# Two hybrid mixer layers on one core: the later modulations computed on VectorE, the neighbourhood projection computed transposed, and buffers redistributed

## The chip, the cores and the metric

One Trainium2 chip; the program runs on one of its cores. The time is device microseconds of one execution, and 2924.19 us is the median of three executions of the kernel before (2923.29 to 2927.37). The engines are named as in the profile: PE is TensorE (matmuls; PEld is its weight load), DVE is VectorE, ACT is ScalarE, POOL is GpSimd, SP is SyncE, which here only issues DMAs. Each engine runs its own instruction list strictly in the order in which it was written.

## The reference, cut to what matters

Two layers over 1024 latent tokens and 256 context tokens, width 1024, all in float32. In each layer:

```python
shift, scale, gate = split(silu(c) @ w_mod + b_mod, 3)      # once for c, once for c_ctx
p = (layer_norm(x) * (1 + scale) + shift) @ w_in            # latent and context tokens
ya = neighbourhood_attention(q_a, k_a, v_a, ...)            # q_a, k_a, v_a are columns of p
yb = latent_attention(...); yc = two_way_linear_scan(...); yd = grouped_query_attention(...)
acc = sum(sigmoid(m[i]) * ((y[i] * silu(z[i])) @ w_branch[i]) for i in range(4))
x = layer_norm(alpha * x + gate * (acc @ w_out)) * ln_g + ln_b
```

The modulation is a product of two vectors (c and c_ctx) with a 1024 x 3072 matrix per layer. Context rows are carried through the first layer only, and the last output is the latent stream.

## The kernel before, in words

Every large matmul is done three times on numbers split into a high and a low part (`whi`/`wlo` for weights, `xh`/`xl` for tokens; `mm_a` keeps the tokens stationary, lines 299 to 301, `mm_b` the weights, lines 307 to 309). `xh` and `xl` hold the normalized, modulated tokens transposed, 8 chunks of 128 channels by 1280 tokens, throughout a layer. `groups` are the token columns 0:256 (context), 256:768 and 768:1280; `qgroups` leaves the context out in layer 1.

A layer has these stages, which give the prefixes of the names in the profile: `g_proj`, `m_proj`, `a_proj` (projections for the three attentions, parts written to DRAM), `lru` (woven into `m_proj` and `a_proj`), `g_att`, `m_att`, `a_att` (attention, with half of the merge gates computed in between and kept in DRAM, name `gates`), `merge`, `outp`. In the trace, layer 0 has `a_proj` from about 255 to 380 us, attention from 410 to 1080, `merge` from 1080 to 1470 and `outp` to 1620; layer 1 has them from 1845 to 1957, 1957 to 2540, 2540 to 2815 and to the end.

Of the modulations, one half of layer 0 is computed at the start, and three pieces are computed beside the merge of layer 0 (prefix `mod`; `later_mods`, line 1165): the gate of layer 0 (1024 columns), shift and scale of layer 1 (2048) and its gate (1024). `modulation` loads `w_mod` in 64 tiles of 128 x 512 (`wm`, tag `q`, three buffers, line 185) and multiplies each on PE in plain float32 with the two conditioning vectors `sc` as a stationary operand of two columns (line 188), gathers over the 8 chunks in PSUM, copies the rows out and transposes them (line 197). `weave` interleaves these steps with those of `merge` in the program's text by shares (line 1011).

`a_steps` (line 801) makes q and k of the neighbourhood attention token tile by token tile, ten tiles of 128 tokens by 512 columns; ACT copies the product out of PSUM into `tmp` (lines 808, 809, q scaled by 0.125), and `put_t` (line 343) transposes four blocks of it on PE (line 348), splits them (`hi_lo`, lines 312 and 313) and writes them to DRAM.

In attention, `values` (line 574) transposes blocks of the probabilities on PE (line 584, PSUM tile `t`), splits them into `ph` (ACT, line 312) and `pl` (DVE, line 313), and multiplies both with the values (lines 591 and 592), two blocks behind (`AHEAD`). Tag `ph` has three buffers, tag `pl` two. `put_u` (line 438) spreads the reciprocal row sums with POOL into `rb` (line 448, one buffer), transposes that on PE (line 464) and multiplies it in. `tmp` is a tag of three buffers that nearly every stage uses. `spare` (line 128) takes buffers of `tmp`, `ph` and `pl` in turn for the residual rows in `outp`.

A scheduling layer below the kernel decides the order in which each engine's instructions finally stand; the order of the text and the buffers are its input.

Of the kernel before, what the change touches and what calls it, by code (L numbers as in the profile page):

```python
# [8 lines left out]
F32 = mybir.dt.float32  # L9
F32R = mybir.dt.float32r  # L10
# [7 lines left out]
KC = D // 128  # L18
# [15 lines left out]
G_LAG = 1  # L34
X_ACT = (0, 2)
M_ORDER = (2, 3, 1, 0)
W_A = 30
W_B = 48
Z_0, GATE_0 = 2, 10
UNITS = [(2, 3), (5, 3), (8, 2)]  # L40
# [7 lines left out]
def hybrid_kernel(ctx: ExitStack, tc, a):  # L48
# [79 lines left out]
    def spare():  # L128

        turns[0] += 1  # L130
        tag = ("tmp", "ph", "tmp", "pl", "tmp", "ph", "pl")[turns[0] % 7]
        return tp.tile([128, 512], F32, tag=tag, name=nm("spare"), bufs=2 if tag == "pl" else 3)

    def bank():
        turns[0] += 1
# [37 lines left out]
    def modulation(l, base, ncols, out, stage, sw):  # L173

        acc = ps_v.tile([128, 512], F32, tag="pv", name=nm("pm"))
        g = 4
        w_ = ncols // g
        n = ncols // 128
        bm = lc.tile([128, 16], F32, tag="bm", name=nm("bm"))
        sp.dma_start(bm[:, :n], a["b_mod"][l, :, base // 128:base // 128 + n])  # L180
        for k in range(KC):
            for h in range(ncols // sw):
                w = stage()
                c0 = base + h * sw
                sp.dma_start(w, a["w_mod"][l, k * 128:(k + 1) * 128, c0:c0 + sw])
                for j in range(sw // w_):
                    q = 32 * (h * sw // w_ + j)
                    pe.matmul(acc[q:q + 2, :w_], sc[:, k, :], w[:, j * w_:(j + 1) * w_],
                              start=k == 0, stop=k == KC - 1)
                yield  # L190
        tps = tbank()
        for j in range(g):
            row = tmp()
            act.copy(row[0:2, :w_], acc[32 * j:32 * j + 2, :w_])
            for i in range(w_ // 128):
                c = j * (w_ // 128) + i
                pe.transpose(tps[:, 2 * c:2 * c + 2], row[0:2, i * 128:(i + 1) * 128], ident[0:2, 0:2])
        mc = lc.tile([128, 2, 16], F32, tag="modc", name=nm("modc"), bufs=4)
        dve.tensor_tensor(mc[:, :, :n].rearrange("p s n -> p n s"),
                          tps[:, :2 * n].rearrange("p (n s) -> p n s", s=2),  # L200
                          bm[:, :n, None].to_broadcast([128, n, 2]), ALU.add)
        if n == 16:
            dve.tensor_scalar(mc[:, :, 8:16], mc[:, :, 8:16], 1.0, None, ALU.add)
        out["m"] = mc
        yield
# [109 lines left out]
    def layer(l, xh, xl, need_ctx, gate, finish, side, ahead=None):  # L315
# [27 lines left out]
        def put_t(dst, t, first, src):  # L343
# [6 lines left out]
            lo = tp.tile([128, 4, 128], F32R, tag="pl", name=nm("tl"), bufs=2)  # L350
# [87 lines left out]
        def put_u(i, c, y, rcp=None):  # L438
# [4 lines left out]
            for g in qgroups:  # L443
                gs = slice(g[0], g[0] + g[1])
                if rcp is not None:
                    r = tp.tile([128, 512], F32, tag="rb", name=nm("rb"), bufs=1)
                    t0, n = g[0] // 128, g[1] // 128
                    pool.tensor_copy(r[:, :g[1]].rearrange("p (t h e) -> p t h e", t=n, h=2),
                                     rcp[:, :, t0:t0 + n].rearrange("p h t -> p t h")[:, :, :, None]
                                     .to_broadcast([128, n, 2, 64]))  # L450
# [123 lines left out]
        def values(o, y, qts, blocks, pts, vt):  # L574
# [5 lines left out]
            def turn(vb, q0, cols):  # L580
# [2 lines left out]
                for i, col in enumerate(cols):  # L583
                    pe.transpose(tb[:, i * 128:(i + 1) * 128], pts[q0 + i][:, col:col + 128], ident)  # L584
                ph = tp.tile([128, 512], F32R, tag="ph", name=nm("ph"), bufs=3)
                pl = tp.tile([128, 512], F32R, tag="pl", name=nm("pl"), bufs=2)
                hi_lo(ph[:, :w], pl[:, :w], tb[:, :w])
                return vb, slice(128 * q0, 128 * q0 + w), ph[:, :w], pl[:, :w]

# [121 lines left out]
        def m_steps():  # L711
# [25 lines left out]
            def second(t, has_q, y, kr):  # L737
# [5 lines left out]
                cl = tp.tile([128, 512], F32R, tag="pl", name=nm("cl"), bufs=2)  # L743
# [56 lines left out]

        def a_steps():
            wa = load_rows(w_in, C_A, 512)
            prev = None
            for t, ps in project(wa, lambda t: 0 if t >= q0t else 256, 512):
                c0 = 0 if t >= q0t else 256
                y = tmp()
                if c0 == 0:
                    act.activation(y[:, :256], ps[:, :256], AF.Copy, scale=0.125)
                act.copy(y[:, 256:], ps[:, 256:])
                if prev:  # L810
                    put_t(*prev)
                prev = qk_a, t, c0 // 128, [y[:, c:c + 128] for c in range(c0, 512, 128)]
                yield
            put_t(*prev)
# [193 lines left out]

        for _ in fill["gen"]:
            pass  # L1010
        weave((f"merge{l}", merge(), 4 * KC * len(qgroups)), (f"mod{l}", side, 68))


        phase[0] = f"last{l}"
# [144 lines left out]
    ctx.push(pools)  # L1159
    x1 = dr.tile([SEQ, D], F32, name="x1", bufs=1)  # L1160

    def raw_w():
        return tp.tile([128, 512], F32, tag="q", name=nm("wm"), bufs=3)
# [107 lines left out]
```

## Time and profile before

| What | Value |
|---|---|
| median of three executions | 2924.19 us |
| the profiled execution | 2926.0 us, span 2924.2 us |
| mean granted TensorE clock | 0.979 of 2.4 GHz |
| PE busy | 2782.2 us, 95% of the span |
| DVE busy | 1503.1 us, 51% |
| ACT busy | 1219.3 us, 42% |
| POOL busy | 420.1 us, 14% |
| HBM traffic | 102 GB/s over the span |

A PE matmul is pipelined: its recorded duration (0.40 us for 512 columns) is longer than the distance to the next start (0.23 us), so costs on PE are read from starts. An idle time is what an engine stood still just before an instruction, with the instruction that released it. PEld waits are those of weight loads, which run ahead of the matmuls and may be hidden.

### The profile page before, as it was taken

The page shows a single profiled execution, that of the slowest core. Times are in us where ns is not written, and L with a number is a line of the kernel's source. Part 1 is how long each engine was busy: PE and PEld are TensorE (multiplying, and loading weights), DVE is VectorE, ACT ScalarE, POOL GpSimd, SP SyncE. Part 2 cuts the span into 40 slices and gives each one's busy share as a digit, 9 for nine tenths or more (in the row PEclk, how much of TensorE's full clock was granted, in tenths as well). Part 3 has the DMA queues.
Part 4 walks back from the last instruction along what each step waited for, and adds up shares of the span by engine and source line. Part 5 has one row for each costly group of instructions (what it writes and reads, how often), then busy time and mean ns, then how long its engine had stood idle before and what let it go on. Part 6 is the DMA issues. An engine that isn't in the chain of part 4 may idle for free. (4 is left out here: it accounts for less than half of the span.)

```text
span 2924.2 us, 40179 instructions
## 1 busy us (share of the span) xinstructions
PE 2782.2 (95%) x14458; PEld 2248.4 (77%) x14458; DVE 1503.1 (51%) x3085; ACT 1219.3 (42%) x2617; POOL 420.1 (14%) x507
## 2 busy tenths in 40 slices
PE   7978999999999999999999797999999999999998
PEld 4766788888888887777767586788888888777776
DVE  5645435555455652233358655445555556533357
ACT  4353535445455552222224435535545455522230
POOL 1211011110111100111222121011111111001131
PEclk9988999999999999999999898999999999999999
DMA  7424232222223324333332333342222333222232
GB/s 249 119 66 146 79 103 84 85 85 85 92 86 124 103 94 128 100 121 120 122 89 87 99 102 102 105 122 87 85 88 78 113 115 110 93 87 88 89 113 88
DMA packets 240424, 301.83 MB, mean 103 GB/s; under 512 B 27488, under 2 KB 160096, under 8 KB 240224
## 3 DMA queue, kind: packets, MB, share of 16 engines
q1 hardware_dynamic: 134368, 225.58, 24.5%
q10 hardware_dynamic: 105856, 73.68, 8.1%
q8 instruction: 114, 1.87, 0.3%
q14 instruction: 86, 0.70, 0.1%
HBM read 217.11 MB, written 82.07 MB: 102 GB/s over the span
## 5 line engine op out<-in xcount | busy, mean ns | idle before, releaser
L307 PE MATMUL merge__mm<-xh,merge__whi 128*128 128x512 f32 (+1 forms) x640 | 242.2, 378 | 0.9 <-ACT a_att__tmp L934 0.9
L308 PE MATMUL merge__mm<-xl,merge__whi 128*128 128x512 f32 (+1 forms) x640 | 238.6, 373 | 0.0
L309 PE MATMUL merge__mm<-xh,merge__wlo 128*128 128x512 f32 (+1 forms) x640 | 238.5, 373 | 0.0
L313 DVE TENSOR_TENSOR m_att__pl<-m_att__t,m_att__ph 128x384 fp32r<-128x384 f32 (+1 forms) x248 | 122.0, 508 | 117.5 <-ACT m_att__ph L312 78.8
L1005 DVE TENSOR_TENSOR merge__tmp<-wide,merge__tmp 128x512 f32<-128x512 f32 (+1 forms) x120 | 76.5, 637 | 194.8 <-PE wide L309 173.7
L263 ACT CAST merge__whi<-merge__wraw 128x256 fp32r<-128x256 f32 (+1 forms) x128 | 65.8, 514 | 249.3 <-PE merge__mm L308 172.9
L1006 POOL TENSOR_TENSOR merge__acc<-merge__acc,merge__tmp 128x512 f32<-128x512 f32 (+1 forms) x60 | 79.0, 1317 | 574.8 <-DVE merge__tmp L1005 574.7
L313 DVE TENSOR_TENSOR g_att__pl<-g_att__t,g_att__ph 128x384 fp32r<-128x384 f32 (+1 forms) x228 | 112.8, 515 | 88.3 <-ACT g_att__ph L312 56.0
L312 ACT CAST m_att__ph<-m_att__t 128x384 fp32r<-128x384 f32 (+1 forms) x248 | 105.2, 440 | 115.0 <-PE m_att__t L584 105.3
L307 PEld LDWEIGHTS merge__mm<-xh,merge__whi 128*128 128x128 f32 x640 | 120.2, 188 | 42.8 <-issue 16.5
L264 DVE TENSOR_TENSOR merge__wlo<-merge__wraw,merge__whi 128x256 fp32r<-128x256 f32 (+1 forms) x128 | 72.0, 563 | 131.8 <-ACT merge__whi L263 124.8
L309 PEld LDWEIGHTS merge__mm<-xh,merge__wlo 128*128 128x128 f32 x640 | 120.3, 188 | 23.8 <-issue 0.4
L308 PEld LDWEIGHTS merge__mm<-xl,merge__whi 128*128 128x128 f32 x640 | 120.3, 188 | 22.4
L307 PE MATMUL wide<-merge__uh,merge__whi 128*128 128x256 f32 (+1 forms) x320 | 127.9, 400 | 9.3 <-DVE merge__tmp L1005 6.7
L312 ACT CAST g_att__ph<-g_att__t 128x384 fp32r<-128x384 f32 (+1 forms) x228 | 98.2, 446 | 83.3 <-PE g_att__t L584 78.7
L307 PE MATMUL a_att__mm<-xh,a_att__whi 128*128 128x512 f32 (+1 forms) x320 | 123.7, 387 | 0.0
L641 DVE TENSOR_SCALAR_CACHE_REDUCE g_att__p<-wide 128x1280 f32<-128x1280 f32 (+1 forms) x72 | 98.6, 1369 | 45.9 <-PE wide L639 35.7
L641 DVE TENSOR_SCALAR_CACHE_REDUCE m_att__p<-wide 128x1280 f32<-128x1280 f32 (+1 forms) x72 | 98.7, 1371 | 42.3 <-PE wide L639 41.8
L309 PE MATMUL a_att__mm<-xh,a_att__wlo 128*128 128x512 f32 (+1 forms) x320 | 120.0, 377 | 0.0
L308 PE MATMUL a_att__mm<-xl,a_att__whi 128*128 128x512 f32 (+1 forms) x320 | 120.0, 375 | 0.0
L308 PE MATMUL wide<-merge__ul,merge__whi 128*128 128x256 f32 (+1 forms) x320 | 119.7, 374 | 0.0
L299 PE MATMUL a_proj__mm<-a_proj__whi,xh 128*128 128x256 f32 (+1 forms) x320 | 110.3, 346 | 9.9 <-ACT a_proj__whi L263 9.8
(418 smaller groups left out, 7908.4 us busy)
## 6 DMA issues: line engine op xcount, KB each, us to landing
merge__wraw<-in_w_chunks_dram SPq DMA_DIRECT2D x64, 256.0 KB, 2.9
mod__wm<-in_w_mod_dram SPq DMA_DIRECT2D x64, 256.0 KB, 3.1
g_proj__wm<-in_w_mod_dram SPq DMA_DIRECT2D x16, 512.0 KB, 9.6
a_att__wraw<-in_w_chunks_dram SPq DMA_DIRECT2D x32, 256.0 KB, 2.8
merge__wraw<-in_w_branch_dram SPq DMA_DIRECT2D x64, 128.0 KB, 2.0
merge__tmp<-start__gates SPq DMA_DIRECT2D x32, 256.0 KB, 3.2
merge__tmp<-outp__gates SPq DMA_DIRECT2D x32, 256.0 KB, 3.4
g_att__wraw<-in_w_chunks_dram SPq DMA_DIRECT2D x28, 256.0 KB, 2.7
```

The lines of the kernel that those rows point to most:

```text
L263: act.copy(hi[:, :n], raw[:, :n])
L264: (pool if by_pool else dve).tensor_sub(lo[:, :n], raw[:, :n], hi[:, :n])
L299: pe.matmul(ps, xh, wh[:, n0:n1], start=first and k == 0, stop=False)
L307: pe.matmul(ps, wh, xh, start=first and k == 0, stop=False)
L308: pe.matmul(ps, wh, xl, start=False, stop=False)
L309: pe.matmul(ps, wl, xh, start=False, stop=last and k == nk - 1)
L312: act.copy(hi, src)
L313: dve.tensor_sub(lo, src, hi)
L641: dve.tensor_scalar(pt[:, :nk], wide[:, :nk], -scale, None, ALU.mult, ALU.min, accum_out=nb)
L1005: dve.tensor_mul(sgm[:, :g[1]], pb[:, :g[1]], sgm[:, :g[1]])
L1006: (pool if w is None else dve).tensor_add(acc[c][:, gs], acc[c][:, gs], sgm[:, :g[1]])
```

## The change

`modulation_apart` replaces `modulation` for the three pieces beside the merge of layer 0 (the piece at the start stays). Each tile of `w_mod` is multiplied on DVE by the two conditioning vectors, one number per partition each, and added into two 128 x 512 sums, which take buffers of tags `ph` and `pl`; after eight tiles, eight matmuls with a single moving column of constants (-0.5) add up the partitions. Sum and factor -2 put the result in the layout that was reached by transposes before. `a_steps` computes q and k transposed at once, weights stationary, for each block of 128 columns and each token group, and splits them directly out of PSUM. Tag `pl` gets a third buffer; `rb` becomes a buffer of `tmp`. The weaving shares change (`W_A`, 68 to 76).

```diff
-W_A = 30
+W_A = 32
-        return tp.tile([128, 512], F32, tag=tag, name=nm("spare"), bufs=2 if tag == "pl" else 3)
+        return tp.tile([128, 512], F32, tag=tag, name=nm("spare"), bufs=3)
+    def modulation_apart(l, base, ncols, out):
+        acc = ps_v.tile([128, 512], F32, tag="pv", name=nm("pm"))
+        n = ncols // 128
+        bm = lc.tile([128, 16], F32, tag="bm", name=nm("bm"))
+        sp.dma_start(bm[:, :n], a["b_mod"][l, :, base // 128:base // 128 + n])
+        for h in range(ncols // 512):
+            sums = [tp.tile([128, 512], F32, tag=tag, name=nm("ms"), bufs=b) for tag, b in (("ph", 3), ("pl", 3))]
+            for k in range(KC):
+                w = raw_w()
+                sp.dma_start(w, a["w_mod"][l, k * 128:(k + 1) * 128, base + h * 512:base + (h + 1) * 512])
+                for s in range(2):
+                    if k == 0:
+                        dve.tensor_scalar(sums[s], w, sc[:, k, s:s + 1], None, ALU.mult)
+                    else:
+                        dve.scalar_tensor_tensor(sums[s], w, sc[:, k, s:s + 1], sums[s], ALU.mult, ALU.add)
+                yield
+            for s in range(2):
+                for c in range(4):
+                    o = s * n + 4 * h + c
+                    pe.matmul(acc[:, o:o + 1], sums[s][:, c * 128:(c + 1) * 128], mhalf[:, 0:1], start=True, stop=True)
+            yield
...
-                pl = tp.tile([128, 512], F32R, tag="pl", name=nm("pl"), bufs=2)
+                pl = tp.tile([128, 512], F32R, tag="pl", name=nm("pl"), bufs=3)
-                    r = tp.tile([128, 512], F32, tag="rb", name=nm("rb"), bufs=1)
+                    r = tmp()
...
             wa = load_rows(w_in, C_A, 512)
-            prev = None
-            for t, ps in project(wa, lambda t: 0 if t >= q0t else 256, 512):
-                c0 = 0 if t >= q0t else 256
-                y = tmp()
-                if c0 == 0:
-                    act.activation(y[:, :256], ps[:, :256], AF.Copy, scale=0.125)
-                act.copy(y[:, 256:], ps[:, 256:])
-                if prev:
-                    put_t(*prev)
-                prev = qk_a, t, c0 // 128, [y[:, c:c + 128] for c in range(c0, 512, 128)]
+            items = [(c, g) for c in range(4) for g in (qgroups if c < 2 else groups)]
+            def part(c, g, ps, ks):
+                xs = xs_g(g)
+                ws = [(wh[:, c * 128:(c + 1) * 128], wl[:, c * 128:(c + 1) * 128]) for wh, wl in wa]
+                mm_b(ps[:, :g[1]], [ws[k] for k in ks], lambda j: xs(ks[j]), ks[0] == 0, ks[-1] == KC - 1)
+            def keep(c, g, ps):
+                n, scale = g[1], 0.125 if c < 2 else 1.0
+                hi = tp.tile([128, 512], F32R, tag="ph", name=nm("th"), bufs=3)
+                lo = tp.tile([128, 512], F32R, tag="pl", name=nm("tl"), bufs=3)
+                act.activation(hi[:, :n], ps[:, :n], AF.Copy, scale=scale)
+                dve.scalar_tensor_tensor(lo[:, :n], ps[:, :n], scale, hi[:, :n], ALU.mult, ALU.subtract)
+                for d, s in enumerate((hi, lo)):
+                    act.dma_start(qk_a[d, c, :, g[0]:g[0] + n], s.bitcast(F32)[:, :n])
+            for c, g in items[:-2]:
+                ps = mm()
+                part(c, g, ps, list(range(KC)))
+                keep(c, g, ps)
                 yield
...
-        weave((f"merge{l}", merge(), 4 * KC * len(qgroups)), (f"mod{l}", side, 68))
+        weave((f"merge{l}", merge(), 4 * KC * len(qgroups)), (f"mod{l}", side, 76))
...
-        yield from modulation(0, 2048, 1024, gate0, raw_w, 512)
-        yield from modulation(1, 0, 2048, mc1, raw_w, 512)
-        yield from modulation(1, 2048, 1024, gate1, raw_w, 512)
+        yield from modulation_apart(0, 2048, 1024, gate0)
+        yield from modulation_apart(1, 0, 2048, mc1)
+        yield from modulation_apart(1, 2048, 1024, gate1)
```

The first place is DVE's list in the first quarter of the merge of layer 0: `merge__acc` is a product that frees a PSUM bank of `wide`, `wlo` a low part of weights, `ms` a sum of the modulation. Before:

```order
L1003 TENSOR_TENSOR merge__acc_10978<-wide,merge__tmp_11058 128x512
L264 TENSOR_TENSOR merge__wlo_11318<-merge__wraw_11315,merge__whi_11317 128x512
L1003 TENSOR_TENSOR merge__acc_11098<-wide,merge__tmp_11099 128x256
L1003 TENSOR_TENSOR merge__acc_11098<-wide,merge__tmp_11113 128x512
L1003 TENSOR_TENSOR merge__acc_11098<-wide,merge__tmp_11127 128x512
```

and the same place now, where `acc_10960` and `acc_11086` are the same two products' targets:

```order
L1053 TENSOR_TENSOR merge__acc_10960<-wide,merge__tmp_11042 128x512
L297 TENSOR_TENSOR merge__wlo_11312<-merge__wraw_11309,merge__whi_11311 128x512
L225 SCALAR_TENSOR_TENSOR mod__ms_11747<-mod__wm_11827,sc,mod__ms_11747 128x512
L1053 TENSOR_TENSOR merge__acc_11086<-wide,merge__tmp_11087 128x256
L225 SCALAR_TENSOR_TENSOR mod__ms_11748<-mod__wm_11827,sc,mod__ms_11748 128x512
L225 SCALAR_TENSOR_TENSOR mod__ms_11747<-mod__wm_11848,sc,mod__ms_11747 128x512
L225 SCALAR_TENSOR_TENSOR mod__ms_11748<-mod__wm_11848,sc,mod__ms_11748 128x512
L1053 TENSOR_TENSOR merge__acc_11086<-wide,merge__tmp_11101 128x512
```

One to three sums now stand between one product and the next; 64 of the 128 sums stand before the end of the merge's first branch.

The second place is SP's list at the beginning of that merge, around the first loads of a branch's result `u`. Before:

```order
L1068 DMA outp__spare_14296<-in_x_dram 128x512
L1068 DMA outp__spare_14448<-in_x_dram 128x512
L278 DMA merge__wraw_11153<-in_w_branch_dram 128x256
L973 DMA merge__tmp_10934<-start__u_25_127 128x256
L973 DMA merge__tmp_10938<-start__u_25_127 128x512
```

and now:

```order
L220 DMA mod__wm_11305<-in_w_mod_dram 128x512
L220 DMA mod__wm_11362<-in_w_mod_dram 128x512
L311 DMA merge__wraw_11137<-in_w_branch_dram 128x256
L220 DMA mod__wm_11434<-in_w_mod_dram 128x512
L220 DMA mod__wm_11483<-in_w_mod_dram 128x512
L1023 DMA merge__tmp_10916<-start__u_25_127 128x256
L1023 DMA merge__tmp_10920<-start__u_25_127 128x512
```

The residual rows (`spare`) were loaded here and are now loaded later; twelve tiles of `w_mod` stand ahead of the first `u`, where three stood before.

The third place is PE's list in `a_proj` of layer 0, at the end of one projection tile. Before:

```order
L299 MATMUL a_proj__mm_2566<-a_proj__whi_2446,xh 128x512
L300 MATMUL a_proj__mm_2566<-a_proj__wlo_2447,xh 128x512
L301 MATMUL a_proj__mm_2566<-a_proj__whi_2446,xl 128x512
L348 MATMUL a_proj__t_2594<-ident,a_proj__tmp_2513 128x128 x4
L307 MATMUL wide<-xh,lru__whi_2530 128x512
```

and now, at the end of one block and the beginning of the next:

```order
L340 MATMUL a_proj__mm_2716<-xh,a_proj__whi_2434 128x512
L341 MATMUL a_proj__mm_2716<-xl,a_proj__whi_2434 128x512
L342 MATMUL a_proj__mm_2716<-xh,a_proj__wlo_2435 128x512
L340 MATMUL a_proj__mm_2747<-xh,a_proj__whi_2392 128x256
L341 MATMUL a_proj__mm_2747<-xl,a_proj__whi_2392 128x256
```

The four transposes between are gone; the product matmuls are as many and as wide in all.

## Rows read from the trace of the kernel before

**Rows 1.** The page's first part: busy us (share of the span) and instructions.

```profile
PE 2782.2 (95%) x14458; PEld 2248.4 (77%) x14458; DVE 1503.1 (51%) x3085; ACT 1219.3 (42%) x2617; POOL 420.1 (14%) x507
```

**Rows 2.** Busy time by stretch: length, PE, PEld, DVE, ACT, POOL, clock, DMA share, GB/s.

```profile
255.00:380.00 125.00, 110.94 (x527) 89.08 (x526) 51.73 (x74) 55.31 (x97) 0.53 (x1) 0.93 0.39 113
1845.00:1957.00 112.00, 109.89 (x622) 93.07 (x620) 44.54 (x57) 49.35 (x83) 0.53 (x1) 1.00 0.30 88
620.00:890.00 270.00, 269.02 (x1579) 227.47 (x1578) 137.62 (x261) 127.42 (x265) 33.73 (x38) 1.00 0.27 87
1080.00:1470.00 390.00, 386.28 (x1930) 288.60 (x1930) 136.16 (x236) 105.22 (x218) 50.18 (x44) 1.00 0.39 119
2540.00:2815.00 275.00, 272.87 (x1144) 212.03 (x1144) 111.22 (x178) 87.79 (x169) 41.70 (x32) 1.00 0.30 94
```

**Rows 3.** Waits of PE from 1080 to 1480 us: total, times, longest.

```profile
PE wide L307 <- DVE merge__tmp L1005: 3.2, 5, 0.8
PE wide L307 <- ACT merge__uh L312: 0.8, 1, 0.8
```

**Rows 4.** Groups of PE instructions, 1080 to 1480 us: busy us, mean ns, idle before.

```profile
L188 PE MATMUL mod__pm<-mod__wm,sc 128*2 128x256 f32 (+1 forms) x192 | 39.6, 449 | 0.3 <-DMA mod__wm<-in_w_mod_dram 0.3
L197 PE MATMUL mod__t<-ident,mod__tmp 2*128 2x2 f32 x32 | 3.9, 209 | 1.2 <-ACT mod__tmp L194 1.1
```

**Rows 5.** Instructions in order of time on PE, merge of layer 0: start, us.

```profile
1095.45 0.60 PE L188 MATMUL mod__pm<-mod__wm,sc 128*2 128x256 f32 x4
1095.98 0.50 PE L307 MATMUL merge__mm<-xh,merge__whi 128*128 128x512 f32 x1
```

**Rows 6.** Instructions in order of time on PE, in `a_proj`.

```profile
305.93 0.60 PE L348 MATMUL a_proj__t<-ident,a_proj__tmp 128*128 128x128 f32 x4
306.28 0.48 PE L307 MATMUL wide<-xh,lru__whi 128*128 128x512 f32 x1
306.60 0.40 PE L308 MATMUL wide<-xl,lru__whi 128*128 128x512 f32 x1
306.84 0.40 PE L309 MATMUL wide<-xh,lru__wlo 128*128 128x512 f32 x1
```

**Rows 7.** The tile of the transposes in `a_proj`: ns min/median/max, first and last start.

```profile
L348 PEld LDWEIGHTS a_proj__t<-ident,a_proj__tmp x76: 137/140/226, 278.2 to 1926.9; 128*128 128x128 f32 x76
```

**Rows 8.** Two lines on DVE: ns min/median/max of one, first and last start.

```profile
L1070 DVE SCALAR_TENSOR_TENSOR outp__Y<-outp__spare,outp__Y x36: 637/686/1120, 1494.2 to 2916.2; 128x512 f32<-128x512 f32 x36
L228 DVE TENSOR_SCALAR g_proj__x<-g_proj__x,g_proj__mv,g_proj__rs x2: 815/815/815, 8.9 to 9.8; 128x1024 f32<-128x1024 f32 x2
```

**Rows 9.** The largest DVE group, 1080 to 1480 us, shapes apart.

```profile
L1005 DVE TENSOR_TENSOR merge__tmp<-wide,merge__tmp 128x512 f32<-128x512 f32 x46 | 31.8, 691 | 108.6 <-PE wide L309 95.6 <-ACT merge__tmp L999 10.2 <-PE merge__mm L309 2.8
```

**Rows 10.** The tile `mod__wm`: issue on SP, and landing.

```profile
L185 SPq DMA_DIRECT2D mod__wm<-in_w_mod_dram x64: 327/333/1623, 1036.1 to 1448.9; - x64
...
DMA to landing us min/median/max: 2.5/3.1/9.1
```

**Rows 11.** Waits of PE from 255 to 380 us.

```profile
PE a_proj__mm L299 <- ACT a_proj__whi L263: 9.8, 4, 6.2
PE a_proj__mm L300 <- DVE a_proj__wlo L264: 3.0, 1, 3.0
```

**Rows 12.** Waits of DVE over the whole span.

```profile
DVE m_att__pl L313 <- PE m_att__pv L592: 23.0, 25, 1.4
DVE g_att__pl L313 <- PE g_att__pv L592: 21.8, 22, 1.7
DVE a_att__pl L313 <- PE a_att__pv L592: 15.3, 23, 1.4
```

**Rows 13.** Waits of weight loads over the whole span.

```profile
PEld m_att__t L584 <- DVE m_att__pl L313: 11.0, 45, 0.8
PEld a_att__t L584 <- DVE a_att__pl L313: 9.5, 38, 0.5
PEld g_att__t L584 <- DVE g_att__pl L313: 8.1, 33, 0.5
```

**Rows 14.** Line 448 (POOL, `rb`): what ended its engine's idle time before it.

```profile
  PE a_att__t L464: 96.1, 9
  PE m_att__t L464: 81.0, 6
```

**Rows 15.** Two lines where POOL and DVE add from SBUF; ns min/median/max.

```profile
L1006 POOL TENSOR_TENSOR merge__acc<-merge__acc,merge__tmp x60: 727/1297/1806, 1203.5 to 2825.3; 128x512 f32<-128x512 f32 x48, 128x256 f32<-128x256 f32 x12
L264 DVE TENSOR_TENSOR merge__wlo<-merge__wraw,merge__whi x60: 415/554/1789, 1079.8 to 1446.8; 128x512 fp32r<-128x512 f32 x30, 128x256 fp32r<-128x256 f32 x30
```

More of the change, by code (lines that the diff above doesn't have):

```diff
@@ L201, in modulation, with raw_w @@
                           bm[:, :n, None].to_broadcast([128, n, 2]), ALU.add)
+        if n == 16:
+            dve.tensor_scalar(mc[:, :, 8:16], mc[:, :, 8:16], 1.0, None, ALU.add)
+        out["m"] = mc
+        yield
+    def raw_w():
+        return tp.tile([128, 512], F32, tag="q", name=nm("wm"), bufs=3)
+    def modulation_apart(l, base, ncols, out):
[18 more added lines that the diff above has]
+                    pe.matmul(acc[:, o:o + 1], sums[s][:, c * 128:(c + 1) * 128], mhalf[:, 0:1], start=True, stop=True)
+            yield
+        mc = lc.tile([128, 2, 16], F32, tag="modc", name=nm("modc"), bufs=4)
+        dve.scalar_tensor_tensor(mc[:, :, :n], acc[:, :2 * n].rearrange("p (s n) -> p s n", s=2), -2.0,
+                                 bm[:, None, :n].to_broadcast([128, 2, n]), ALU.mult, ALU.add)
         if n == 16:
@@ L349, in put_t @@
             hi = tp.tile([128, 4, 128], F32R, tag="ph", name=nm("th"), bufs=3)
-            lo = tp.tile([128, 4, 128], F32R, tag="pl", name=nm("tl"), bufs=2)
+            lo = tp.tile([128, 4, 128], F32R, tag="pl", name=nm("tl"), bufs=3)
             p3 = pt.rearrange("p (a b) -> p a b", a=4)
@@ L742, in second @@
                 ch = tp.tile([128, 512], F32R, tag="ph", name=nm("ch"), bufs=3)
-                cl = tp.tile([128, 512], F32R, tag="pl", name=nm("cl"), bufs=2)
+                cl = tp.tile([128, 512], F32R, tag="pl", name=nm("cl"), bufs=3)
                 hi_lo(ch[:, b0 * 128:384], cl[:, b0 * 128:384], pt[:, b0 * 128:384])
@@ L802, in a_steps @@
             wa = load_rows(w_in, C_A, 512)
-            prev = None
-            for t, ps in project(wa, lambda t: 0 if t >= q0t else 256, 512):
-                c0 = 0 if t >= q0t else 256
-                y = tmp()
-                if c0 == 0:
-                    act.activation(y[:, :256], ps[:, :256], AF.Copy, scale=0.125)
-                act.copy(y[:, 256:], ps[:, 256:])
-                if prev:
-                    put_t(*prev)
-                prev = qk_a, t, c0 // 128, [y[:, c:c + 128] for c in range(c0, 512, 128)]
-                yield
-            put_t(*prev)
+            items = [(c, g) for c in range(4) for g in (qgroups if c < 2 else groups)]
[15 more added lines that the diff above has]
+                keep(c, g, ps)
+                yield
+            last = [(c, g, mm()) for c, g in items[-2:]]
+            for k in range(KC):
+                for c, g, ps in last:
+                    part(c, g, ps, [k])
+            for c, g, ps in last:
+                keep(c, g, ps)
+                yield
             wv = load_rows(w_in, C_AV, 256)
@@ L1160, in hybrid_kernel @@
     x1 = dr.tile([SEQ, D], F32, name="x1", bufs=1)
-    def raw_w():
-        return tp.tile([128, 512], F32, tag="q", name=nm("wm"), bufs=3)
     def later_mods():
-        yield from modulation(0, 2048, 1024, gate0, raw_w, 512)
-        yield from modulation(1, 0, 2048, mc1, raw_w, 512)
-        yield from modulation(1, 2048, 1024, gate1, raw_w, 512)
+        yield from modulation_apart(0, 2048, 1024, gate0)
+        yield from modulation_apart(1, 0, 2048, mc1)
+        yield from modulation_apart(1, 2048, 1024, gate1)
     def fin0(t, Y, later):
```

## The prediction

> **What bounds the kernel.** I read the busy shares first: PE is busy for 95% of the span, no other engine for more than 51% [rows 1]. Then the stretches, because a mean hides stages: in the merge of layer 0 PE is busy 386.3 of 390 us, in the attention stretch shown 269.0 of 270 and in the second `a_proj` 109.9 of 112; only in the first `a_proj` does it stand still for 14 us of 125 [rows 2]. The granted clock is 1.00 (2.4 GHz) in all of these but the first `a_proj`, at 0.93. So wherever the change acts, the time is PE's list, and DVE and ACT have room: in the merge of layer 0 DVE is busy 136.2 of 390 us. Third, the waits of PE in that merge: 3.2 us for DVE and 0.8 us for ACT [rows 3]. An edit there is worth the PE time it takes out, less the new time in which PE waits for DVE.
>
> **The modulations leave PE.** Their 96 matmuls (192 records, two each) and the small transposes behind them cost PE 39.6 and 3.9 us [rows 4], with nothing beside them on that engine. One place shows that this is real distance and not only modelled length: from the first modulation matmul at 1095.45 to the next product at 1095.98 [rows 5]. Gain: 43.5 us.
>
> In their place come 64 matmuls (eight sums groups, two vectors, four blocks) with one moving column and a stationary block of 128 x 128 float32. No row shows that shape. The nearest are the float32 transposes of 128 x 128 blocks: four take from 305.93 to 306.28, and the first product behind them is 0.32 us to the next start where the usual distance is 0.24 (306.60 to 306.84), so 0.43 us for four, 0.11 each [rows 6]. The lower end is therefore 64 x 0.11 = 7 us. The weight load of such a block takes 0.14 us [rows 7], and a float32 product stands as two records, so the upper end is 128 x 0.14 = 18 us. I take two records of 0.11 each, 14 us, because the transposes are a single pass. Net gain on PE: 29.5 us.
>
> **What it puts on DVE.** 64 tiles times two: 112 adds at 0.686 us and 16 first multiplications, for which the nearest row is 0.815 us for twice the width, say 0.41 [rows 8]; together 83.4 us. DVE would be busy 136 + 83 = 220 of some 360 us, 61%. Today it stands still 95.6 us before the products of line 1005 alone, waiting for PE [rows 9], so there is room on the mean. It is not free: behind a sum stand the products that free a bank of `wide` and a buffer of `tmp`, and PE waits for those; the order above has one to three sums between two products, and half of all sums fall into the first of four branches. A pair is 1.37 us; three banks of `wide` cover about that much (three products of 6 x 0.23 = 1.4 us each). Also a sum waits for its tile: one tile lands 3.1 us after issue [rows 10], with three buffers one every (3.1 + 1.4) / 3 = 1.5 us, hardly slower than DVE uses them. And SP, which issues in order, now holds the first `u` loads behind twelve tiles; PE has the first gate products (24 x (0.12 + 0.23 + 0.23) = 14 us) to do meanwhile. I put 4 us for all of this, as much as PE's waits there now, with 0 and 20 as ends.
>
> **`a_proj` without transposes.** 76 transposes x 0.11 = 8.4 us off PE [rows 6, 7]; 38 copies leave ACT, which has room in any case. The product matmuls are the same columns. Against it: in layer 0 PE starves for weights at the beginning, 9.8 + 3.0 us [rows 11], and what it can do on two banks while they come falls from two blocks of 512 columns (24 x 0.46 = 11.0 us) to one of 256 and one of 512 (24 x 0.35 = 8.4 us): 2.6 us more. And a bank is now free only when DVE, which has long `lru` work in its list, has made the low part, where before two ACT copies freed it: 2 us for both layers, between 0 and 8. Net gain 3.8 us; ends: 8.4 gained, 2.2 lost.
>
> **The third `pl` buffer.** DVE waited 60.1 us in 70 places for the product that still read an old `pl` [rows 12]; that wait goes. What PE could get from it is the waiting of its weight loads for `pl`, 28.6 us in 116 places, none longer than 0.8 [rows 13]. Most of it runs while earlier matmuls still stream (PE is busy 269.0 of 270 us), and most of what DVE waits for besides is ACT's `ph`, which stays. I take 6 us gained; ends 28.6 gained and 5 lost, the loss because the scheduler orders all stages anew.
>
> **`rb` in `tmp`.** 30 spread rows now hold one of three `tmp` buffers from POOL's copy until PE's transposes; POOL has stood 96.1 us in 9 cases and 81.0 in 6 for the old row's release [rows 14], so such a row is held for some 10 us while gates and values use the other two. I put 2 us lost, ends 0 and 12. `spare`: at the merge's start its `ph` and `pl` are now taken, so residual rows come later; they feed DVE in `outp`, not PE. Zero, up to 3 if a row comes late, covered otherwise by DVE's own work there.
>
> **Sum**, against the profiled execution of 2926.0 us: -43.5 + 14 + 4 - 3.8 - 6 + 2 = -33.3, so 2892.7. The median shown lies 1.8 us below that execution, so I forecast 2891 us. From here on, times are for the median; a difference under 0.2%, 5.8 us, is no change that can be measured.
>
> **A rule weighed.** POOL's adds from SBUF take 1.30 us at the median but up to 1.81, and DVE's `wlo`, 0.69 us for 512 columns when alone, up to 1.79 [rows 15]: now and then the two hold each other up. The Trainium skill, "SBUF — State Buffer", section "Who interferes with whom", says that a VectorE instruction with two SBUF inputs and a GpSimd instruction that reads SBUF exclude each other for a whole instruction. The trace agrees with it in these two maxima. By that rule the 112 adds, whose inputs are both in SBUF, collide with POOL's 36 adds of this merge; if each of the 36 held DVE up for a whole add of 1.3 us, DVE would have 47 us more and stand at 267 of 360 us, and the sum would stay as it is as long as PE does not wait. It speaks for the slower rival below.
>
> **Rivals.**
> - *VectorE's list becomes the bound of this merge* (slower). The place is the first branch and a half, where sums stand between products. Price: 64 pairs x 1.37 = 88 us, if each stood before a product that PE needs at once. Without my 4 us the rest of the sum is -37.3; from 37 of these 88 us on, nothing is left. With two thirds, 59 us, it is 2946. For it: half of the sums crowd into the first branch, SP is blocked behind them, and POOL collides. Against: 61% busy on the mean, three banks of slack, PE waits of 3.2 us now. Chance 0.06.
> - *`tmp` is too short in attention.* If each of the 30 spread rows costs PE half a microsecond more and the third `pl` buffer gives nothing, 15 - 2 + 6 = 19 us are lost against the forecast: 2910. For it: the long holds in rows 14. Against: POOL's copy can wait without PE waiting. Chance 0.16.
> - *The third `pl` buffer gives all of its 28.6 us.* 22.6 us better: 2868. For it: 116 places of 0.2 to 0.3 us, each on the way of a transpose. Against: hidden under streaming matmuls. Chance 0.15.
> - *PE time taken out does not move the end*, because the merge is held by its weights' arrival: about 2920. Against: PE has no wait on weights in that merge, and DMA is 39% busy [rows 2]. Chance 0.05.
>
> The forecast keeps 0.58. Range 2864 to 2914: it takes in the second and third rival, leaves out the first and the last (0.11) and some of the tails. Faster: 0.58 + 0.16 + 0.15 = 0.89; same 0.05; slower 0.06.
>
> **What would show it.** Right: in the merge of layer 0 no modulation matmuls on PE but 64 of about 0.2 us; the merge shorter by 20 to 30 us, ending near 1435 if the earlier stages give their share; DVE there near 220 us busy; PE's waits for DVE under 10 us; each `a_proj` some 2 us shorter; DVE's waits for `pv` gone. Wrong: waits of PE on lines 1053 and 1055 of tens of microseconds in the first branch; sums that wait for `wm` in front of products; small matmuls over 0.3 us apart; attention stages longer than before with waits on `tmp`.

## The result, and the profile after

| Kernel | median us | runs | ratio to before, with 95% interval |
|---|---|---|---|
| before | 2925.0 | 4 | 1 |
| changed | 2886.8 (2885.07 to 2891.05) | 4 | 0.9871 [0.9854, 0.9888] |

The change takes 38 us off, faster by 1.3%; 2891 was forecast, within 2864 to 2914. The number is right. Most of the terms behind it are not, and the experiments show how their errors made up for each other.

The page of the changed kernel, first part (columns as in [rows 1]):

```profile
PE 2729.4 (95%) x14334; PEld 2253.0 (78%) x14334; DVE 1578.9 (55%) x3215; ACT 1202.3 (42%) x2569; POOL 416.8 (14%) x507
```

PE lost 53 us of busy time, where the terms of the forecast take off 37.9, and DVE gained 76, where they add 83. The span lost 41 us. Where, is read from the first matmul of each stage in both profiled executions. Each column is one execution; `outp` of layer 0 alone is 2.4 to 3.1 us shorter than in this execution of before in six of the runs below that leave its matmuls as they were, so the small differences mean little:

| Stage | before us | after us | difference |
|---|---|---|---|
| up to the end of the first `a_proj` | 411.4 | 393.9 | -17.5 |
| three attentions, layer 0 | 670.9 | 664.7 | -6.2 |
| merge, layer 0 (modulations) | 391.4 | 385.5 | -5.9 |
| `outp`, layer 0 | 156.7 | 155.4 | -1.3 |
| projections, layer 1 | 329.6 | 323.1 | -6.5 |
| three attentions, layer 1 | 580.0 | 575.7 | -4.3 |
| merge and `outp`, layer 1 | 384.2 | 385.0 | +0.8 |

The merge, on which most of the forecast rested (-25.5), gave 5.9; the stages up to the end of the first `a_proj` (2 forecast) gave 17.5. The busy times of the changed kernel by stretch, columns as in [rows 2] (its stretches for `a_proj` and the merge, both of layer 0):

```profile
255.00:394.00 139.00, 129.18 (x736) 110.17 (x734) 55.59 (x86) 52.81 (x88) 0.53 (x1) 0.99 0.35 112
1058.50:1444.00 385.50, 364.89 (x1841) 302.98 (x1840) 212.28 (x353) 102.16 (x212) 52.34 (x44) 0.97 0.42 120
```

In the second row PE now stands still for 20.6 of 385.5 us, where it stood still for 3.7 of 390, and the granted clock is 0.97 where it was 1.00. The first row shows the opposite: 0.93 has become 0.99. What PE waits for in the merge of layer 0 of the changed kernel, columns as in [rows 3] (its lines 340, 1053 and 1055 are 307, 1003 and 1005 of before):

```profile
PE wide L340 <- DVE merge__acc L1053: 11.3, 5, 9.1
PE wide L340 <- DVE merge__tmp L1055: 6.5, 7, 2.1
PE wide L340 <- ACT merge__uh L345: 2.0, 1, 2.0
```

One wait of 9.1 us is nearly half. DVE in order of time just there (start, duration, line, operation; in brackets the idle time before it and what ended it):

```profile
1156.61 1.41 DVE L225 SCALAR_TENSOR_TENSOR mod__ms<-mod__wm,sc,mod__ms 128x512 f32<-128x512 f32 x2
1167.47 0.75 DVE L225 SCALAR_TENSOR_TENSOR mod__ms<-mod__wm,sc,mod__ms 128x512 f32<-128x512 f32 x1 [9.46 <-DMA mod__wm<-in_w_mod_dram]
1168.14 0.69 DVE L1053 TENSOR_TENSOR merge__acc<-wide,merge__tmp 128x512 f32<-128x512 f32 x1
```

The product of line 1053, for which PE waits, stands in DVE's list behind a sum whose tile has not come. SP's issues in order of time show what that tile stands behind:

```profile
1153.75 0.43 SPq L1067 DMA_DIRECT2D last__gate<-mod__modc  x1
1154.62 0.34 SPq L220 DMA_DIRECT2D mod__wm<-in_w_mod_dram  x1
1155.00 0.43 SPq L1067 DMA_DIRECT2D last__gate<-mod__modc  x1
1155.94 2.43 SPq L220 DMA_DIRECT2D mod__wm<-in_w_mod_dram  x2
```

And the transfers issued in that stretch, 1152 to 1170 us (count, size of one, median us from issue to landing):

```profile
mod__wm<-in_w_mod_dram SPq DMA_DIRECT2D x3, 256.0 KB, 12.8
last__gate<-mod__modc SPq DMA_DIRECT2D x2, 4.0 KB, 12.0
```

The two stores of the finished gate vector (line 1067) are 4 KB each, in 1024 pieces of 4 bytes; they take 12 us at the median, and the three tiles beside them 12.8, where 2.8 is usual. The kernel before had the same stores, and its latest tile, 9.1 us [rows 10], was the first tile of `w_mod` issued behind them:

```profile
1181.99 1.05 SPq L1017 DMA_DIRECT2D last__gate<-mod__modc  x2
1185.30 0.34 SPq L185 DMA_DIRECT2D mod__wm<-in_w_mod_dram  x1
```

But there it was PE's own matmuls that used the tiles, and they waited 0.3 us for them in all [rows 4].

The clock is the second loss. PE in order of time, two groups of the new one-column matmuls and the products behind the second:

```profile
1072.55 1.84 PE L230 MATMUL mod__pm<-mhalf,mod__ms 128*128 128x1 f32 x16
1074.25 0.48 PE L340 MATMUL merge__mm<-xh,merge__whi 128*128 128x512 f32 x1
...
1239.55 7.86 PE L230 MATMUL mod__pm<-mhalf,mod__ms 128*128 128x1 f32 x48
1247.28 0.77 PE L340 MATMUL wide<-merge__uh,merge__whi 128*128 128x512 f32 x1
1247.85 0.63 PE L341 MATMUL wide<-merge__ul,merge__whi 128*128 128x512 f32 x1
```

Sixteen records take 1.70 us, 0.106 each; 48 at that price are 5.1 us, but they took 7.73, and the products behind them start first 0.57 and then 0.43 us apart in place of 0.23. The stretches around the long stop and behind the 48, columns as in [rows 2]:

```profile
1158.00:1163.00 5.00, 1.81 (x9) 1.18 (x7) 0.01 (x1) 0.90 (x2) 0.00 (x0) 1.00 0.49 34
1163.00:1173.00 10.00, 4.12 (x13) 3.54 (x14) 4.97 (x9) 0.00 (x0) 0.00 (x0) 0.53 0.56 95
...
1243.00:1252.00 9.00, 9.00 (x32) 8.03 (x33) 3.43 (x8) 0.63 (x1) 0.94 (x1) 0.50 0.12 37
1252.00:1258.00 6.00, 5.56 (x26) 4.28 (x26) 6.00 (x9) 1.63 (x3) 2.45 (x2) 0.97 0.37 109
```

The clock falls to 1.2 GHz (0.50) while PE stands still for 9 us, and again 3 us after the start of the 48 small matmuls, where PE counts as busy for every microsecond. Read in steps of 1 us, there is a third fall, of 3.4 us, from 1064.6 us on, at the end of a stop of 2.0 us for ACT. The three falls are 24 us; less the 5 of them in which PE stood still, PE worked for some 19 us at half the clock, an estimated loss of 9 us.

Of the signs of being right that the prediction named, three came: the small matmuls take 0.21 us for two records, DVE is busy for 212 us in the merge, and its waits for `pv` are gone from its list. Three did not: the merge is not 20 to 30 us shorter (it ends at 1444, not near 1435), PE's waits for DVE are not under 10 us, and the first `a_proj` is far more than 2 us shorter. Of the signs of being wrong, a sum that waits for `wm` in front of a product came, and small matmuls 0.32 us apart for two records, in the group of 48.

### The profile page after: what moved, and what is told of

Its sections match the earlier page's. It is cut to its first block, busy times and chain, and to the rows that moved or that the text cites. A ratio compares the mean times of both kernels' runs of the same rounds, so it can differ in the third digit from the quotient of the medians.

```text
span 2883.3 us, 39659 instructions
## 1 busy us (share of the span) xinstructions
PE 2729.4 (95%) x14334; PEld 2253.0 (78%) x14334; DVE 1578.9 (55%) x3215; ACT 1202.3 (42%) x2569; POOL 416.8 (14%) x507
## 3 DMA queue, kind: packets, MB, share of 16 engines
q1 hardware_dynamic: 134368, 225.58, 25.1%
## 5 line engine op out<-in xcount | busy, mean ns | idle before, releaser
L340 PE MATMUL wide<-merge__uh,merge__whi 128*128 128x256 f32 (+1 forms) x320 | 129.4, 404 | 29.6 <-DVE merge__tmp L1055 14.1
L342 PE MATMUL wide<-merge__uh,merge__wlo 128*128 128x256 f32 (+1 forms) x320 | 119.2, 373 | 0.0
```

Of the source, the lines that this page charges most:

```text
L340: pe.matmul(ps, wh, xh, start=first and k == 0, stop=False)
L342: pe.matmul(ps, wl, xh, start=False, stop=last and k == nk - 1)
```

## The experiments

Each was timed beside the kernel before; its medians there were 2923.9, 2925.2 and 2926.6, so ratios are compared rather than medians.

| Run | median us | ratio to before | difference us |
|---|---|---|---|
| 1 buffers alone | 2908.0 | 0.9939 [0.9925, 0.9954] | -18 |
| 2 projection alone | 2911.1 | 0.9954 [0.9942, 0.9967] | -13 |
| 3 changed, modulations back on PE | 2893.8 | 0.9892 [0.9878, 0.9905] | -32 |
| 4 changed, gate in rows | 2874.6 | 0.9826 [0.9812, 0.9840] | -51 |
| 5 spread rows alone | 2920.9 | 0.9988 [0.9977, 0.9998] | -4 |
| 6 changed, gate on ACT's queue | 2881.5 | 0.9856 [0.9834, 0.9877] | -42 |
| 7 gate in rows, early | 2873.0 | 0.9827 [0.9813, 0.9840] | -51 |
| 8 as 7, sums in one tag | 2863.5 | 0.9792 [0.9775, 0.9810] | -61 |
| 9 share 32 alone | 2934.6 | 1.0025 [1.0015, 1.0034] | +7 |
| 10 projection, share 30 | 2915.9 | 0.9964 [0.9951, 0.9976] | -11 |
| 11 modulations alone, best form | 2892.6 | 0.9884 [0.9869, 0.9899] | -34 |

(The difference is the ratio less 1, times 2925.)

### 1 and 5: the buffers

Run 1 is the kernel before with both edits below, the first at all four places of tag `pl`; run 5 has the second edit alone.

```diff
-                pl = tp.tile([128, 512], F32R, tag="pl", name=nm("pl"), bufs=2)
+                pl = tp.tile([128, 512], F32R, tag="pl", name=nm("pl"), bufs=3)
-                    r = tp.tile([128, 512], F32, tag="rb", name=nm("rb"), bufs=1)
+                    r = tmp()
```

> The kernel before with the buffers alone: a third buffer for low parts, the spread sums among the temporaries; projection and modulations as before (before: 2925.0 us). Forecast's terms: -6 + 2, so 2921. Theory T, from the two traces: the six attention stages together were 9 us shorter after the whole change, and PE's stop of 6.2 us at 268 us in the first a_proj was ACT's cast of a weight, queued behind a cast that waited for the store of an old low part; both go with the third buffer, with some 2 us of slow clock behind the stop: -17, so 2908. Rival R: the stop went because the new projection asks for its weights earlier; then only the attention's 9 us go: 2916.

> The kernel before (2923.9) with the spread sums in the temporaries alone, low parts still in two buffers. Forecast's term: 2 lost, so 2926. With both buffer edits the kernel took 2908.0, 16 less. Theory L: all of it is the third low-part buffer, worth 18, and this run is 2926. Rival B: POOL no longer stands 96.1 and 81.0 us for the old row's release, so rows are ready earlier and PE's transposes of them wait less: up to 10 of the 16 come from here, 2914.

Run 1 came out at 2908.0, the number of theory T, but not for its reason. The stop in the first `a_proj` is still there (PE's waits from 245 to 280 us in run 1):

```profile
PE a_proj__mm L299 <- ACT a_proj__whi L263: 5.2, 1, 5.2
```

That part of T falls. The six attention stages became 12 us shorter (from the first matmuls: 3.6 + 2.8 + 1.6 + 0.3 + 1.7 + 1.9); the rest, 6 us net, came in pieces of up to 3.3 us from the other stages. What left PE's path is seen in its weight loads, here of run 1 over the whole span (columns as in [rows 13]):

```profile
PEld m_att__t L584 <- DVE m_att__pl L313: 8.3, 30, 0.8
PEld a_att__t L584 <- DVE a_att__pl L313: 6.5, 24, 0.5
...
PEld g_att__t L584 <- DVE g_att__pl L313: 5.6, 23, 0.3
...
PEld g_att__pv L592 <- DVE g_att__pl L313: 1.1, 5, 0.3
```

In the kernel before the first three were 28.6 us in 116 places [rows 13]; now they are 20.4 in 77. The products behind them waited for `pl` too, and the transposes of the spread rows for `rb`; more rows of the kernel before, same view (`pv` of `a_att`, not shown, has 2.0 us):

```profile
PEld g_att__pv L592 <- DVE g_att__pl L313: 3.9, 17, 0.3
...
PEld m_att__pv L592 <- DVE m_att__pl L313: 3.6, 16, 0.5
PEld m_att__t L464 <- POOL m_att__rb L448: 3.4, 6, 0.6
...
PEld a_att__t L464 <- POOL a_att__rb L448: 2.1, 6, 0.5
...
PEld g_att__t L464 <- POOL g_att__rb L448: 1.5, 3, 0.5
```

With both edits the waits of the products for `pl` fall from 9.5 to 1.6 us, but those for ACT's `ph` grow from 9.5 to 13.7. The waits for `rb`, 7.0 us, are gone from the list, in run 5 as in run 1. Run 5 refutes the sign of the `rb` term: the spread rows in `tmp` cost nothing and gave some 4 us. POOL, no longer held by the old row [rows 14], writes the next one early. The third `pl` buffer is then worth the rest, 18 - 4 = 14 us; alone it was not run.

### 2, 9 and 10: the projection

Run 2 puts the new `a_steps` with its share into the kernel before, run 10 the new `a_steps` alone, run 9 the share alone:

```diff
-W_A = 30
+W_A = 32
```

> The kernel before with the transposed projection alone (two buffers for low parts, spread sums in their own buffer, modulations on PE). Forecast's term: -3.8, so 2921. After the whole change the two a_proj stages with what is woven into them were 17.5 and 6.5 us shorter, 24 in all, where 8.4 are the transposes. Theory T (the third buffer took the stop at 268 us away): at most -14, 2911 or above. Rival R (the projection itself took it away): near -24, 2901.

> The kernel before (2924.5, middle of its medians) with the weaving share of the projections at 32 in place of 30, nothing else. The projection alone, which had this share too, took 12.8 us off, of which the forecast's transposes explain 8.4 less 4.6. Theory P: the transposed projection itself removes PE's waits for weights (6.2 us at 268, 8 us around 366), since PE can work on a column block of a few weights without a transpose and its copies in between; the share alone is worth nothing: 2922 to 2927. Theory W: the share sets when the weights of the projection are asked for (234 us with it, 245 without); it takes the stop at 268 by itself: 2914 to 2918.

> The transposed projection alone, as in the second experiment (2911.1), but with the share left at 30. Theory P: 2911 again, within 2. Theory W: the part that the share brought is missing; 2917 to 2921.

PE's waits from 245 to 280 us, first in run 2, then in run 10:

```profile
PE a_proj__mm L307 <- DVE a_proj__tl L815: 2.8, 1, 2.8
PE wide L299 <- ACT m_proj__ch L312: 1.5, 1, 1.5
```

```profile
PE a_proj__mm L307 <- ACT a_proj__whi L263: 7.7, 1, 7.7
```

With the share at 30 the stop for the weights stays; with 32 it goes, as theory W has it. Run 2 came out at the number of the theory that gave the third buffer the credit for this, but the stop went there with two buffers. Run 9 shows that the share alone loses 7 us: there the stop at 268 is gone too, and PE waits later in that stage instead. Its waits from 255 to 417 us:

```profile
PE wide L307 <- ACT lru__lrug L515: 4.1, 6, 1.3
PE wide L639 <- ACT lru__lrug L515: 3.0, 1, 3.0
PE a_proj__mm L300 <- DVE a_proj__wlo L264: 2.9, 2, 1.9
PE a_proj__mm L299 <- ACT a_proj__whi L263: 2.9, 2, 2.1
```

In layer 1 of run 9 PE also stands still for 6.1 us at once before the old transposes, for ACT's copy. So neither theory stands alone. The projection by itself gives 11 us. The transposes are most of it: in the stages `m_proj` and `a_proj` of both layers PE is busy for 9.0 us less in run 10 than before, where 8.4 were forecast. The waits for the projection's weights around 366 us [rows 11], 6.5 us, are gone at either share. In their place came waits for the low part `tl`, which DVE must make before a bank is free. In the changed kernel, who waited for it (total, times):

```profile
  PE a_proj__mm L340: 4.7, 3
  PE lru__mm L340: 2.5, 1
  PE a_proj__mm L332: 0.9, 1
```

These are 8.1 us (8.4 in run 2, 7.2 in run 10), and the kernel before had none. The share gives some 3 more with the new projection and takes 7 in the old one: ratios 0.9954 and 0.9964 have intervals that overlap, so the 3 are not certain. Why the old projection suits 32 so badly was not taken further.

### 3 and 11: the modulations

Run 3 is the changed kernel with the old `modulation` for the three pieces. Run 11 is the kernel before with the new modulations alone, in the form of run 8.

> The changed kernel (2886.8) with the later modulations computed on PE as before (share 68 again), everything else as changed. Forecast's terms: modulations are worth -43.5 + 14 + 4 = -25.5, so this should be 2912. Theory M, from the trace: the merge of layer 0 became only 5.9 us shorter, because of what the sums brought (a PE stop of 9.1 us at 1160 behind a sum whose tile landed 14.1 us after issue, slow clock after it and after 48 one-column matmuls at 1240, more waits for DVE): this should be 2893. Rival: the modulations on PE also fare worse in the new order, since wm tiles are then late as well: 2900 to 2912.

> The kernel before with the modulations on DVE alone, in their best form: both sums of a piece in the high-part buffers, the gate turned into rows and stored early. Forecast's terms for the modulations: -43.5 + 14 + 4 = -25.5, so 2899 against 2924.5. Rival N: in the kernel before, with its two low-part buffers and other order, DVE is late more often, and PE's waits for it are 10 us or more: 2908 and above.

Run 3: as built, the modulations on DVE are worth 7 us (2893.8 less 2886.8; by the ratios 6, with intervals that just overlap), not 25.5, as theory M had it. Run 11: in their best form they are worth 34; rival N falls. The merge was 364.1 us there (391.4 before): 27.3 less, close to the 25.5 forecast, with 31.4 us less of PE's busy time, where 29.5 were forecast. `outp` was 4.0 us shorter, but hardly for the modulations: in runs 1, 2, 3, 5, 9 and 10, which have them on PE, it was shorter by 2.4 to 3.1 too. What the other 3 us came from was not taken apart.

### 4, 6, 7 and 8: what the modulations lost

Run 4 turns the gate on PE before it is stored; run 6 leaves it and moves the store to another queue:

```diff
-            sp.dma_start(gd[s].rearrange("(k p) -> p k", p=128), gate["m"][:, s, :KC])
+            pt, row = tbank(), tmp(128)
+            pe.transpose(pt[:KC, :128], gate["m"][:, s, :KC], ident)
+            act.copy(row[:KC, :128], pt[:KC, :128])
+            sp.dma_start(gd[s].rearrange("(k p) -> k p", p=128), row[:KC, :128])
```

```diff
-            sp.dma_start(gd[s].rearrange("(k p) -> p k", p=128), gate["m"][:, s, :KC])
+            act.dma_start(gd[s].rearrange("(k p) -> p k", p=128), gate["m"][:, s, :KC])
```

> The changed kernel with the gate vector turned on PE into rows of 128 before its store to DRAM, so that the store has 8 pieces of 512 bytes in place of 1024 of 4 bytes. Theory S: the scattered stores (9 to 15 us to landing) stand in the same queue ahead of the tile on which DVE's sum waited 9.5 us; with them gone PE's stop of 9.1 us and the 2 us of slow clock behind it go: 2876. Rival W: the tile would have been late anyway, because SP issues it late or its buffer comes free late: within 2 us of 2886.8. The forecast had nothing for this store.

> The changed kernel (2886.8) with the gate's scattered stores (2048 pieces of 4 bytes) issued on ACT's queue in place of SP's, where the w_mod tiles are. Theory Q: the tile was late because it stood behind the stores in its own queue; on another queue it passes them: 2876, as with the store in rows (2874.6). Theory P: the 16 DMA engines are busy with the small pieces whichever queue they come from; the tile is late by half or more of what it was, PE stops for 4 to 9 us: 2881 to 2887.

Issue to landing of the 64 tiles of `w_mod` in run 4 and, in the second fence, in run 6:

```profile
DMA to landing us min/median/max: 2.6/2.8/4.5
```

```profile
DMA to landing us min/median/max: 2.5/2.8/10.7
```

Theory S stands: without the scattered stores no tile is late, and 12 us come back (2886.8 to 2874.6). On ACT's queue a tile was still 10.7 us under way and PE stood still 6.4 us at once in the profiled execution. That speaks for theory P: the tile did not pass the stores on another queue. The Trainium skill, "DMA: Bandwidth & Descriptors", section "Queues, rings and completion order", says that each DMA engine serves the queues that have work in turn, a packet at a time; by that rule a second queue shares with the small pieces and does not pass them. The 10.7 us, between 14.1 and 4.5, agree with it. What the late tile cost in time there stays open: the four times scatter from 2873.4 to 2890.6, the median 2881.5 lies at the lower end of theory P's range, and the profiled execution, with its stop of 6.4 us, is the quickest of the four.

Run 7 turns and stores the gate inside the merge; run 8 changes one word of it:

```diff
-            sums = [tp.tile([128, 512], F32, tag=tag, name=nm("ms"), bufs=b) for tag, b in (("ph", 3), ("pl", 3))]
+            sums = [tp.tile([128, 512], F32, tag=tag, name=nm("ms"), bufs=b) for tag, b in (("ph", 3), ("ph", 3))]
```

> As the kernel with the gate in rows (2874.6), but turned and stored as soon as the gate is there, inside the merge. There the store came at 1440 us, DVE waited 16.1 us for the loaded gate and outp was 4.9 us longer than in the changed kernel. Theory: these come back, 2870. Rival: the transposes and the copy, put into the merge, cost PE waits of their own: 2873 to 2877.

> As the last kernel, but both sums of a piece in the buffers of the high parts (three), so that DVE cannot run two pieces ahead and PE gets the one-column matmuls in eight groups of 16 records, never 48 or 32 together. Theory C (slow clock behind the large groups): with the gate in rows the granted clock was 0.60, 0.88 and 0.83 in three windows of 10 us around them, 4.0 + 1.2 + 1.7 = 6.9 us lost; they come back: 2863 if the last kernel is 2870. Theory D: the groups are harmless (their 0.11 us each stays the same) and the sums now wait for PE to free a buffer: 0 to 5 us slower than the last kernel.

Run 7 does not differ measurably from run 4 (ratios 0.9827 and 0.9826). In the profiled executions `outp` is 4.6 us shorter, as the theory had it, but the times do not show it; whether the early turn gives anything stays open. Run 8 is 9.5 us faster than run 7, and the intervals do not touch. Its merge, and PE's waits from 1060 to 1430 us (its lines 348, 1061 and 1063 are 340, 1053 and 1055 of the changed kernel):

```profile
1060.00:1426.00 366.00, 356.69 (x1835) 296.00 (x1834) 219.99 (x354) 104.06 (x216) 54.94 (x44) 1.00 0.40 123
```

```profile
PE wide L348 <- DVE merge__tmp L1063: 6.5, 12, 1.2
PE wide L348 <- ACT merge__uh L353: 2.7, 2, 1.5
PE wide L348 <- DVE merge__acc L1061: 0.8, 1, 0.8
```

The small matmuls stand in groups of 16 records. DVE is busy for 220 us, and PE waits 7.3 us for it, in 13 short pieces. From the first matmul of the merge to that of `outp` it is 366.3 us, 25.1 less than before. That is what was forecast for the change as it stood.

Theory C has the direction right, but it accounts for about a third of the 9.5 us. The clock of 1.00 is a mean: read in steps of 1 us, PE had 0.50 for 10 us of the merge in run 7 and for 3.4 us in run 8. The first two lines are run 7, its 48 records and the stretch behind them; the others are run 8, one group of 16 and what followed:

```profile
1230.03 5.41 PE L230 MATMUL mod__pm<-mhalf,mod__ms 128*128 128x1 f32 x48
1235.00:1239.00 4.00, 4.00 (x13) 3.22 (x14) 2.54 (x7) 0.00 (x0) 0.05 (x1) 0.57 0.22 66
...
1319.95 1.84 PE L230 MATMUL mod__pm<-mhalf,mod__ms 128*128 128x1 f32 x16
1322.96 0.79 PE L348 MATMUL wide<-merge__uh,merge__whi 128*128 128x512 f32 x1 [1.17 <-DVE merge__tmp L1063]
1322.50:1326.50 4.00, 3.54 (x9) 2.85 (x10) 3.43 (x8) 1.65 (x3) 0.94 (x1) 0.57 0.62 166
```

So the 48 took 5.3 us in run 7, 0.110 a record, and the clock fell only behind them; and it fell once in run 8 too, after a group of 16 and a stop of 1.2 us. In run 11 it did not fall at all in the merge. In the profiled executions the merge of run 8 is 3.5 us shorter than that of run 7, about what the clock explains, and `outp` is 3.0 us shorter; where the rest of the 9.5 comes from is not shown. Run 8, 2863.5 us, is the fastest kernel of the study, 23 us faster than the changed one.

## Why the prediction was right, and where its steps were wrong

| Step | forecast us | measured us |
|---|---|---|
| modulations | -25.5 | -7 as built (run 3), -30 in the form of run 8 (run 8 less run 3), -34 alone (run 11) |
| projection | -3.8 | -13 (run 2) |
| third `pl` buffer | -6 | -14 (runs 1 and 5) |
| `rb` in `tmp` | +2 | -4 (run 5) |
| sum | -33.3 | -38 |

- *The modulations off PE, 43.5 us.* Right: less the new matmuls it is 29.5 us, and PE's busy time in the merge of run 11 is 31.4 us less. The new matmuls: 128 records of 0.106 us, 13.6 us at full clock against 14 forecast. The tile of the sums in the changed kernel:

```profile
L230 PE MATMUL mod__pm<-mhalf,mod__ms x128: 164/250/353, 1072.5 to 1342.5; 128*128 128x1 f32 x128
L225 DVE SCALAR_TENSOR_TENSOR mod__ms<-mod__wm,sc,mod__ms x112: 736/744/1779, 1043.9 to 1283.5; 128x512 f32<-128x512 f32 x112
```

- *"I put 4 us for all of this"* is the step that failed. PE stood still for 20.6 us in the merge, 17 more than before, of which it waited 17.8 for DVE, and the slow clock came on top. The bounds (0 to 20) held the waits alone. The reasoning named the right mechanism, a sum that waits for its tile in front of a product; but it took 3.1 us as the price of a tile, although [rows 10] shows 9.1 as the longest. The row with the maximum was there, and its cause, the scattered stores ahead of that tile, could have been read from the trace of before.
- *The clock* was in no term, at an estimated 9 us. That one-column matmuls cost 0.106 us held for the groups of 16 in the changed kernel (1.70 us each); of the 48 together the clock fell in the middle in the changed kernel (0.161) and behind them in run 7 (0.110).
- *`a_proj`.* The transposes' 8.4 us are borne out (9.0 in run 10). Of the costs put against them, the one for the banks came, and larger: 8 us of waits for DVE's low part where 2 were put, at the end of the range given (8). The other side was missing: the waits for weights around 366 us went with the projection, and the one at 268 us with the share of 32. The -13 us hold errors of both signs.
- *The third buffer.* Mechanism right, size off by more than two: 14 us where 6 were put, within its bounds. *`rb`*: wrong sign. Both were judged by what PE's busy share hides (269.0 of 270 us in [rows 2]); yet the short waits of weight loads were on the path to a good part. That DVE's 60.1 us of waiting for old `pl` go is right as well, but its waits for ACT's `ph` in the three attentions grew by 59 us in run 1, from 155.7 to 214.6, so DVE itself was hardly earlier.
- *The rivals.* The slower one, VectorE's list as the bound, did happen in kind (PE waited for DVE), at 18 us instead of the 59 it asked for, and half of that was one late tile. The second (`tmp` too short) is refuted by run 5. The third (28.6 us from the buffer) came half way. The fourth is refuted by runs 8 and 11: of 29.6 and 31.4 us of PE time taken out of the merge, 25.1 and 27.3 came off its length.
- *The rule weighed.* DVE was busy for 212.3 us in the merge against 220 forecast, but 15 of the 128 sums ran before it, and all of them took 98.9 us against 83.4: an add took 0.744 us at the median where 0.686 was put, and nine took 1.1 to 1.8. Each of the nine began while an instruction of POOL ran. Eight are adds with both inputs in SBUF, held up as "SBUF — State Buffer", "Who interferes with whom" in the Trainium skill says. The nine cost some 8 us above the medians, not the 47 that the rule allowed.

The number of the forecast was right by luck: a loss of 18.5 us on the modulations and gains of 23 us on the other terms were both missed, and nearly cancelled.

## What to carry to other kernels

When work moves from the bounding engine to one that this engine waits for, read the maximum and not the median of every transfer that the new work waits for, and look for what shares its queue: two stores of 4 KB in pieces of 4 bytes cost 12 us here. Small matmuls with one moving column were cheap in groups of 16 between wide ones; a row of 48 was followed or cut by the slow clock in runs 4, 6, 7 and the changed kernel alike. And a sum that hits is no proof of its terms: put each part alone on the chip before believing the explanation.

## What the hardware showed that was not expected

- PE busy without a gap for 8 us with one-column matmuls, and yet the granted clock fell from 1.00 to 0.50 for 10 us; with groups of 16 records it stayed at 1.00 through the merge of run 11 and fell once, for 3.4 us, in that of run 8.
- A store of 4 KB in 4-byte pieces landed after 9 to 15 us and took tiles of 256 KB beside it from 2.8 to 14.1 us, and to 10.7 when the stores were on another queue.
- Waits of PE's weight loads of 0.2 to 0.3 us each, under a PE that is busy for 99.6% of the stretch, were in good part real time: with 8 us of them gone before transposes, 8 before products and 7 for `rb`, and 4 more for ACT's `ph`, the six attention stages were 12 us shorter.
